# A hybrid transformer block on one core: weight sums taken one from the other, own tiles for four u columns, E tables on VectorE alone, output tables of the scan built in a later stage

## The chip, the core and the metric

The kernel runs on one core of a Trainium2 chip. The metric is the device time of one execution in microseconds (us). The core has a matrix engine (TensorE, PE in the rows; PEld are its weight loads), VectorE (DVE), ScalarE (ACT), GpSimd (POOL) and a queue engine (SP) that here issues every transfer in program order.

## The reference, cut to what matters

One layer on 1024 latent tokens and 256 context tokens, model width 1024, in float32:

```python
x = half_step_ffn(x, mods[0:3], ffn1_g_pre, ffn1_g_post, ffn1_w_gu, ffn1_w_down)
ctx = half_step_ffn(ctx, mods_c[0:3], ...same weights...)
disc = [s5_discretise(...) for d in range(2)]          # scan tables of 32 groups, 64 states
p = modulate(rms_norm(x, mix_g_pre), mods[3], mods[4]) @ w_in     # and the same for ctx
bg, cg, v, u = split(p)
y_conv = bg * grid_short_conv(cg * v, conv_w)
y_ssm = s5_readout(u, s5_states(u, disc, h0s), disc, ssm_d, w_glu, b_glu)
x = x + mods[5] * rms_norm(concat([y_conv, y_ssm]) @ w_out, mix_g_post)
x = half_step_ffn(x, mods[6:9], ffn2_g_pre, ffn2_g_post, ffn2_w_gu, ffn2_w_down)
# half_step_ffn: h @ w_gu -> g, u (2816 each); (silu(g) * u) @ w_down; norm, gate, add
```

## The kernel before

The latents' two FFNs use a seven-product scheme (Strassen's kind) on 2x2 blocks: for each *feature tile* f (128 columns of g and the same of u, 22 tiles) and each product m = 1 to 7, `g_lat` (L661) makes one weight operand of 128x512 in `prep` (L737) and multiplies it with a combination of the tokens' blocks in `prod` (L767). With g0, g1 the two row halves of a g tile and u0, u1 of a u tile, the operand is g0 for m=1, g1 for m=2, u0+u1 for m=5, u0+u1-g0 for m=6, g1-(u0+u1-g0) for m=3, g0-u0 for m=7, u1 for m=4. An operand is normally split into a high part (copied by ScalarE, `w<-t` or `w<-wr`) and a low part (VectorE, `w<-t,w`), and a product is 12 matmuls.

At the start of each FFN the normed tokens are not yet split, so the first four features run their products 1, 2, 5, 3 (the *early* ones, in the order m by m) with unsplit float32 operands: 4 matmuls each, in two passes, so 8 rows a product (`ps<-z,wr` for m=1 and 2, `ps<-z,t` for m=5 and 3). Meanwhile VectorE combines and splits the tokens' blocks (*hops*, rows `z<-z,z` and `z<-z`). Raw weights lie in four rotating buffers `wr` of 512 KB; the first FFN gives the four early u tiles buffers of their own (`z`, by `apart_u=True`, loaded by `u_load`), the second reloads them into `wr`.

`self.sums` holds u0+u1 of a feature; for the early features it is dropped after each use:

```python
                if m == 3 or f < ne:
                    sums.pop(f)
```

Around the products run other pieces of work as *fill* (generators that are stepped between products; `SP` sets how many fill steps pass between two steps of `s5_params`):

- `s5_params` (L1180 on) during the latents' first FFN makes the tables of the scan. Its last big part is the E table: 8 blocks of 6 operations of 128x512 (`tb<-tb`), the even blocks on VectorE, the odd ones on GpSimd. All blocks use the same two buffers, and each half is stored to DRAM (`pd<-tb`, 256 KB).
- `s5_prep` (L1399) during the context's first FFN (`g_ctx`, 128x256 matmuls) makes the B tables, then small transfers that lay out a Toeplitz table (`gd<-z`, `td<-gd`), then the output (C) tables: 4 blocks of 6 operations of 128x1024 (`z<-z,z`), alternately on VectorE and GpSimd, each with two stores of 512 KB (`pd<-z`).
- `u_lat` (L1501) projects the latents to u: 8 groups of 24 matmuls; beside it the context's tokens are normed, transposed and split (`ctx_in`, rows `z<-z,sy`, then `ps<-ident,z`, then `z<-t,z`). After it come `u_ctx` and the scan's pairs, which read the tables from `pd`.

Most of the order of instructions on each engine comes from the tile framework's scheduler; at the start of the first FFN VectorE and TensorE keep the program's order.

Of the kernel before, what the change touches and what calls it, by code (L numbers as in the profile page):

```python
# [68 lines left out]
class Kernel:  # L69
# [111 lines left out]
    def setup(self):  # L181
# [16 lines left out]
        self.pd = self.t(dr, [PAIRS, P, TO], "pd")  # L198
        self.pwd = self.t(dr, [P, D], "pwd")
        self.brd = self.t(dr, [P, D], "brd")  # L200
        self.gd = self.t(dr, [H, G, 15, H], "gd")
        self.td = self.t(dr, [P, G, P], "td")
        self.ud = self.t(dr, [G * H, T8, CL], "ud")
# [456 lines left out]
    def g_lat(self, wgu, hb, hr, sd, fills, early, late, held, apart_u=False):  # L660
# [73 lines left out]
        def prep(f, m):  # L734
            v = {
                side + str(q): raws[f, side][:, 4 * q : 4 * q + 4, :].rearrange("p k n -> p (k n)")
                for side in A[m] for q in range(2)  # L737
            }
            if m in (1, 2, 4):
                x = v[{1: "g0", 2: "g1", 4: "u1"}[m]]  # L740
            elif m == 7:
                x = self.t2()
                self.sub(x, v["g0"], v["u0"])
            else:
                x = sums.get(f)
                if x is None:
                    x = sums[f] = self.t2()
                    self.add(x, v["u0"], v["u1"])
                    have = 5
                else:  # L750
                    have = at_sum[f]
                if m in (6, 3) and have == 5:
                    self.sub(x, x, v["g0"])
                    have = 6
                if m == 3:
                    self.sub(x, v["g1"], x)
                    have = 3
                at_sum[f] = have
                if m == 3 or f < ne:
                    sums.pop(f)  # L760
            wops[f, m] = x if (f, m) in early else self.wop(x)

# [74 lines left out]
        def prepare(n, eager=True):  # L837
            nonlocal done
            while done < min(n, len(seq)):
                fetch(done)  # L840
                if any((seq[done][0], side) not in raws for side in A[seq[done][1]]):
                    break
                prep(*seq[done])
                done += 1
                if eager:
                    fetch(None)
# [327 lines left out]
    def s5_params(self):  # L1174
# [160 lines left out]
        for b in range(8):  # L1335
            gs = slice(4 * b, 4 * b + 4)
            er, ei, xt = (
                u.rearrange("p (a m n) -> p a m n", a=4, m=4) for u in (ee[:, :512], ee[:, 512:], arena[:, :512])
            )
            shp = [P, 4, 4, 32]  # L1340
            x0 = e32[0][:, gs, :].unsqueeze(2).to_broadcast(shp)
            x1 = e32[1][:, gs, :].unsqueeze(2).to_broadcast(shp)
            v0 = vv[:, 0, :, gs].rearrange("p m a -> p a m").unsqueeze(3).to_broadcast(shp)
            v1 = vv[:, 1, :, gs].rearrange("p m a -> p a m").unsqueeze(3).to_broadcast(shp)
            self.cmul(er, ei, x0, x1, v0, v1, xt, pl if b % 2 else None)
            for r, m in ((0, er), (1, ei)):
                c0 = EO + 256 * r
                self.load(
                    pdv[:, 2 * b : 2 * b + 2, c0 : c0 + 256], m.rearrange("p (a q) m n -> p a (q m n)", q=2)
                )  # L1350
            yield
# [30 lines left out]
    def s5_prep(self):  # L1382
# [82 lines left out]
        for t in range(T8):  # L1465
            r = slice(t * H, t * H + H)
            self.load(self.td[r], self.gd[:, :, 7 - t : 15 - t].rearrange("h g l k -> h g (l k)"))
            if t % TY == TY - 1:
                yield
        for o in range(4):  # L1470
            gs = slice(8 * o, 8 * o + 8)
            mr, mi, xt = slot(shp), slot(shp), slot(shp)
            prb, pib = power(1, 0, gs), power(1, 1, gs)
            cr_ = ct[:, 0, gs, :].unsqueeze(2).to_broadcast(shp)
            ci_ = ct[:, 1, gs, :].unsqueeze(2).to_broadcast(shp)
            e = pl if o % 2 else None
            self.mul(mr, cr_, prb, e)
            self.mul(xt, ci_, pib, e)
            self.add(mr, mr, xt, e)
            yield  # L1480
            self.mul(mi, ci_, prb, e)
            self.mul(xt, cr_, pib, e)
            self.sub(mi, mi, xt, e)
            for r, m in ((0, mr), (1, mi)):
                c0 = CO + 256 * r
                self.load(
# [228 lines left out]
    def run(self):  # L1715
# [199 lines left out]
        u = self.tb.rearrange("p (g c) -> p g c", g=G)  # L1915
        cx = ctx_in()
        next(cx)
        for _ in itertools.chain(self.u_lat(mhi, mlo, 0, u), self.u_lat(mhi, mlo, 1, u)):
            next(cx, None)
        for _ in cx:  # L1920
            pass
        self.u_ctx(chi2, clo2)
# [100 lines left out]
        order2 = [(f, m) for m in (1, 2, 5, 3) for f in range(4)]  # L2023
        tb = [self.ta() for _ in range(3)]
        held = {f: {1: halves(tb[f])[0], 2: halves(tb[f])[1], 0: [tb[f]]} for f in range(3)}
        ffn = self.g_lat(i["ffn2_w_gu"][0], hb, hr, self.sd[1], (0, 0, 1, 1, 0, 1, 0), order2, 3, held)
        next(ffn)
        for _ in range(4):
            self.g_fetch()
# [10 lines left out]
        ss.append(spl(3))  # L2040
        acc = self.out_group(ss[2], wo2)
        next(p)
        ssa = self.squares(part[:4])
        for _ in range(4):
            self.g_prep()
# [15 lines left out]
        self.eager = True  # L2061
        for _ in range(4):
            self.g_prod(4, 8)
        bl[1] = self.normer(part[4:], ssa, *ab)
        for _ in range(4):
            self.g_prod(4, 99)
        act = dict(h=lambda: next(h), p=lambda: self.g_prod(4, 99))
# [52 lines left out]
FW = 22  # L2120
FN = (2, 2, 1, 1, 2, 2, 2)
GAP = 6
SP = (1, 2)
UN2 = 3
EARLY2 = 4
TAIL = 3
# [47 lines left out]
```

## Time and profile before

| | us |
|---|---|
| three runs | 2076.4, 2077.2, 2079.46 (median 2077.2) |
| profiled execution, own time | 2077.89 |
| its span (first to last instruction) | 2076.1 |
| TensorE busy | 1961.8 (94%) |
| VectorE busy | 1433.3 (69%) |
| ScalarE / GpSimd busy | 825.3 / 191.3 |

The span is what the rows cover; 1.8 us of the execution's own time lie outside it. The share of busy time is an average over stages with different limits, so the places where TensorE waits are read one by one.

### The profile page before, as it was taken

What the parts mean: (1) busy time and instruction counts of PE and PEld (TensorE: products, weight loads), DVE (VectorE), ACT (ScalarE), POOL (GpSimd) and SP (SyncE); (2) the same over time, 40 slices, a digit from 0 to 9 for tenths busy, and PEclk for the clock granted to TensorE, in tenths of its full rate; (3) what the DMA queues carried; (4) which work ended last, traced back from release to release, by engine and by line L of the source; (5) the groups of instructions that cost most, each with busy time, mean ns of one, the idle gap of its engine ahead of it and who ended that gap; (6) DMA issues with size and microseconds to landing.
All of it is one profiled execution on the core that took longest, in us unless ns stands there. A gap on an engine that the chain in (4) does not pass through costs nothing. (4 is left out here: it accounts for less than half of the span.)

```text
span 2076.1 us, 25812 instructions
## 1 busy us (share of the span) xinstructions
PE 1961.8 (94%) x9364; PEld 1562.7 (75%) x9364; DVE 1433.3 (69%) x2532; ACT 825.3 (40%) x1459; POOL 191.3 (9%) x106
## 2 busy tenths in 40 slices
PE   7899999989898999999998899997999999999997
PEld 3477778867898877777887778763788888887775
DVE  1874469787766679787528985486865555577977
ACT  5433333423343345566532334353333333334543
POOL 0000000040347000000003430010000000000000
PEclk9999999999999999999999999999999999999999
DMA  9167632445579977476665533134632322267554
GB/s 325 31 218 249 240 137 72 132 127 167 172 222 268 294 249 251 147 259 224 180 207 170 182 112 122 53 130 122 203 122 81 100 73 82 87 254 267 198 182 162
DMA packets 334059, 356.78 MB, mean 172 GB/s; under 512 B 47024, under 2 KB 248428, under 8 KB 333932
## 3 DMA queue, kind: packets, MB, share of 16 engines
q1 hardware_dynamic: 331628, 346.75, 51.4%
q10 hardware_dynamic: 2304, 8.39, 1.0%
q8 instruction: 73, 1.20, 0.2%
q14 instruction: 54, 0.44, 0.1%
HBM read 282.97 MB, written 74.17 MB: 172 GB/s over the span
## 5 line engine op out<-in xcount | busy, mean ns | idle before, releaser
L51 PE MATMUL ps<-z,w 128*128 128x512 f32 (+1 forms) x5328 | 1151.2, 377 | 39.6 <-DVE w L51 13.1
L51 PEld LDWEIGHTS ps<-z,w 128*128 128x128 f32 x5328 | 937.7, 192 | 236.4 <-DVE w L51 14.9
L51 PE MATMUL ps<-w,w 128*128 128x512 f32 x1848 | 427.3, 392 | 16.3 <-DVE w L51 9.7
L51 PEld LDWEIGHTS ps<-w,w 128*128 128x128 f32 x1848 | 346.4, 188 | 95.6 <-DVE w L51 14.7
L51 ACT ACTIVATE w<-wr 128x512 fp32r<-128x512 f32 (+1 forms) x270 | 206.6, 767 | 348.4 <-PE ps L51 281.7
L51 DVE TENSOR_TENSOR w<-wr,w 128x512 fp32r<-128x512 f32 (+1 forms) x264 | 246.9, 937 | 117.4 <-ACT w L51 110.8
L51 ACT ACTIVATE w<-t 128x512 fp32r<-128x512 f32 x292 | 177.1, 626 | 213.4 <-DVE t L51 129.9
L51 DVE TENSOR_TENSOR w<-t,w 128x512 fp32r<-128x512 f32 x292 | 198.6, 691 | 77.0 <-ACT w L51 76.6
L51 DVE TENSOR_TENSOR t<-t,ps 128x512 f32<-128x512 f32 x150 | 102.4, 684 | 97.6 <-PE ps L51 94.5
L51 PE MATMUL ps<-z,t 128*128 128x512 f32 x512 | 148.0, 449 | 11.4 <-DVE t L51 10.3
L51 ACT ACTIVATE t<-ps 128x512 f32<-128x512 f32 (+2 forms) x143 | 77.4, 542 | 166.3 <-PE ps L51 162.8
L51 PEld LDWEIGHTS ps<-z,t 128*128 128x128 f32 x512 | 96.8, 190 | 60.8 <-issue 36.2
L51 ACT ACTIVATE w<-z 128x512 fp32r<-128x512 f32 x110 | 69.6, 632 | 146.2 <-PE ps L51 144.0
L51 DVE TENSOR_TENSOR z<-z,z 128x512 fp32r<-128x512 f32 (+3 forms) x127 | 106.6, 869 | 15.5 <-ACT z L51 11.6
L51 DVE TENSOR_TENSOR t<-wr 128x512 f32<-128x512 f32 x140 | 94.2, 686 | 32.2 <-DMA wr<-in_ffn_w_gu 18.1
L51 ACT ACTIVATE t<-z 128x1024 bf16<-128x1024 f32 (+3 forms) x132 | 75.5, 605 | 47.2 <-DVE z L51 30.8
L51 DVE TENSOR_TENSOR w<-z,w 128x512 fp32r<-128x512 f32 x110 | 75.5, 686 | 26.6 <-ACT w L51 26.4
L51 POOL TENSOR_TENSOR z<-z,z 128x1024 f32<-128x1024 f32 x24 | 79.2, 3320 | 76.3 <-PE ps L51 42.0
L51 ACT ACTIVATE t<-t 128x512 f32<-128x512 f32 (+1 forms) x83 | 51.7, 623 | 78.6 <-DVE t L51 78.2
L51 DVE TENSOR_TENSOR z<-t,ps 128x512 f32<-128x512 f32 (+1 forms) x52 | 29.8, 573 | 64.9 <-PE ps L51 64.3
L51 POOL TENSOR_TENSOR tb<-tb 128x512 f32<-128x512 f32 x24 | 33.6, 1412 | 435.4 <-DMA sd<-z 409.0
L51 ACT ACTIVATE z<-z 128x512 fp32r<-128x512 f32 (+2 forms) x76 | 48.3, 673 | 56.7 <-DVE z L51 56.7
(121 smaller groups left out, 1402.1 us busy)
## 6 DMA issues: line engine op xcount, KB each, us to landing
wr<-in_ffn_w_gu SPq DMA_DIRECT2D x146, 512.0 KB, 4.1
wr<-in_ffn_w_down SPq DMA_DIRECT2D x198, 256.0 KB, 4.2
tb<-in_w_ada SPq DMA_DIRECT2D x56, 512.0 KB, 4.5
sd<-z SPq DMA_DIRECT2D x44, 512.0 KB, 3.0
z<-sd SPq DMA_DIRECT2D x88, 256.0 KB, 5.4
wr<-in_ffn_w_down SPq DMA_DIRECT2D x22, 512.0 KB, 4.9
wr<-in_w_in SPq DMA_DIRECT2D x20, 512.0 KB, 4.0
z<-in_w_ada SPq DMA_DIRECT2D x16, 512.0 KB, 6.3
```

Of the source, the lines that this page charges most:

```text
L51: r = f(*a, **kw)
```

## The change

Five parts. (1) In `prep` an early feature keeps its sum from m=5 on: m=3 works it over in place (two operations, before three), and m=6 is made back from m=3's result (one operation, before two). A new condition in `prepare` holds m=3 and m=6 back until the products that read the tile were issued. (2) The second FFN gets `apart_u=True` too: its first four u tiles are loaded early into buffers of their own. (3) The E table is made on VectorE alone, in halves of three operations, with two fill steps between halves. (4) The C tables move from `s5_prep` into a new generator `s5_ctab` that is stepped beside `u_lat`, all on VectorE; its inputs go through DRAM (a new `ctd`, 512 KB, and half of `pwd`). (5) In the second FFN the last four token tiles are scaled by ScalarE instead of VectorE.

```diff
+        self.ctd = self.t(dr, [P, D], "ctd")
...
+                if m == 6 and have == 3:
+                    self.sub(x, v["g1"], x)
+                    have = 6
                 if m in (6, 3) and have == 5:
                     self.sub(x, x, v["g0"])
...
-                if m == 3 or f < ne:
+                if m == (6 if f < ne else 3):
                     sums.pop(f)
...
-                if any((seq[done][0], side) not in raws for side in A[seq[done][1]]):
+                f, m = seq[done]
+                if any((f, side) not in raws for side in A[m]):
+                    break
+                if f < ne and m in (3, 6) and left[f] & {5, 3 if m == 6 else 5}:
                     break
...
-            self.cmul(er, ei, x0, x1, v0, v1, xt, pl if b % 2 else None)
+            self.mul(er, x0, v0)
+            self.mul(xt, x1, v1)
+            self.sub(er, er, xt)
+            yield
+            self.mul(ei, x0, v1)
+            self.mul(xt, x1, v0)
+            self.add(ei, ei, xt)
...
+        self.load(self.ctd, ct.rearrange("p r a h -> p (r a h)"))
+
+    def s5_ctab(self):
+        slot = lambda shape: self.t(self.zp, shape, "z")
+        pw, ct = slot([P, 2, T8, 32]), slot([P, 2, 32, H])
+        self.load(pw.rearrange("p r t a -> p (r t a)"), self.pwd[:, 512:])
+        self.load(ct.rearrange("p r a h -> p (r a h)"), self.ctd)
...
         for o in range(4):
...
-            e = pl if o % 2 else None
-            self.mul(mr, cr_, prb, e)
-            self.mul(xt, ci_, pib, e)
-            self.add(mr, mr, xt, e)
+            self.mul(mr, cr_, prb)
+            self.mul(xt, ci_, pib)
+            self.add(mr, mr, xt)
             yield
...
+        ctab = self.s5_ctab()
         for _ in itertools.chain(self.u_lat(mhi, mlo, 0, u), self.u_lat(mhi, mlo, 1, u)):
             next(cx, None)
+            next(ctab, None)
...
-        ffn = self.g_lat(i["ffn2_w_gu"][0], hb, hr, self.sd[1], (0, 0, 1, 1, 0, 1, 0), order2, 3, held)
+        ffn = self.g_lat(i["ffn2_w_gu"][0], hb, hr, self.sd[1], (0, 0, 1, 1, 0, 1, 0), order2, 3, held, True)
...
+        for _ in range(4):
+            self.u_load()
...
-        bl[1] = self.normer(part[4:], ssa, *ab)
+        self.scale(part[4:], self.rsq(ssa), nc.scalar)
+        bl[1] = self.blocks(part[4:], *ab)
...
-SP = (1, 2)
+SP = (1,)
```

How it moves instructions is shown at three places, all on VectorE.

First FFN, from the last u sum of m=3 on (`t` are the operands, `z_265` an own u tile, `wr` raw weights, `ps` products). Before:

```order
L51 TENSOR_TENSOR t_232_677<-z_265 128x512
L51 TENSOR_TENSOR t_232_677<-t_232_677,wr_5_76 128x512
L51 TENSOR_TENSOR t_232_677<-wr_5_76,t_232_677 128x512
L51 TENSOR_TENSOR tb_72<-tb_72,ps_683 128x512
L51 TENSOR_TENSOR t_235_694<-t_222_640,ps_689 128x512
L51 TENSOR_TENSOR z_541<-z_541 128x512
L51 TENSOR_TENSOR z_697<-z_540,z_697 128x512
L51 TENSOR_TENSOR z_700<-z_541,z_700 128x512
L51 TENSOR_TENSOR t_238_703<-wr_5_76 128x512
L51 TENSOR_TENSOR t_238_703<-t_238_703,wr_2_73 128x512
L51 TENSOR_TENSOR w_706<-t_238_703,w_706 128x512
```

Now:

```order
L51 TENSOR_TENSOR t_217_617<-t_217_617,wr_5_76 128x512
L51 TENSOR_TENSOR t_217_617<-wr_5_76,t_217_617 128x512
L51 TENSOR_TENSOR tb_72<-tb_72,ps_676 128x512
L51 TENSOR_TENSOR t_232_687<-t_223_641,ps_682 128x512
L51 TENSOR_TENSOR z_542<-z_542 128x512
L51 TENSOR_TENSOR z_690<-z_541,z_690 128x512
L51 TENSOR_TENSOR z_693<-z_542,z_693 128x512
L51 TENSOR_TENSOR t_194_521<-wr_2_73,t_194_521 128x512
L51 TENSOR_TENSOR w_697<-t_194_521,w_697 128x512
```

The sum ahead of m=3 (`t_232_677<-z_265`) and the one ahead of m=6 (`t_238_703<-wr_5_76`) are gone; the adds of products (`<-...,ps`) stand where they stood.

Beside `u_lat`, around the scale of the context's two token tiles (`TENSOR_SCALAR z<-z,sy`; `z_8453,z_8452` are the inputs of the C tables, `w` a weight split, `z_8377<-t` the context's split). Before:

```order
L51 SCALAR_TENSOR_TENSOR sy_8598<-sq_8596,sy_8597 128x2
L51 TENSOR_SCALAR z_7802<-z_7802,sy_8598 128x1024
L51 TENSOR_SCALAR z_7803<-z_7803,sy_8598 128x1024
L51 TENSOR_TENSOR w_8635<-wr_4_75,w_8634 128x1024
L51 TENSOR_TENSOR w_8818<-wr_5_76,w_8817 128x1024
L51 TENSOR_TENSOR z_8435<-t_1374_8690,z_8433 128x256
```

Now:

```order
L51 TENSOR_TENSOR z_8632<-z_8632,z_8634 128x1024
L51 SCALAR_TENSOR_TENSOR sy_8554<-sq_8553,sy_8551 128x2
L51 TENSOR_TENSOR z_8634<-z_8453,z_8452 128x1024
L51 TENSOR_TENSOR sq_8553<-sy_8554 128x2
L51 SCALAR_TENSOR_TENSOR sq_8553<-sq_8553,sv_8550 128x2
L51 SCALAR_TENSOR_TENSOR sy_8555<-sq_8553,sy_8554 128x2
L51 TENSOR_SCALAR z_7744<-z_7744,sy_8555 128x1024
L51 TENSOR_SCALAR z_7745<-z_7745,sy_8555 128x1024
L51 TENSOR_TENSOR w_8841<-wr_2_73,w_8840 128x1024
L51 TENSOR_TENSOR z_8377<-t_1366_8664,z_8375 128x256
L51 TENSOR_TENSOR z_8633<-z_8453,z_8452 128x1024
L51 TENSOR_TENSOR z_8709<-z_8453,z_8452 128x1024
```

Sixteen of the 24 C operations and two weight splits now stand between the context's residual and its scale, seven more between its first and last splits.

Second FFN, where the operands of m=3 are made (`t_1941`, `t_1947`, `t_1950` before; now `t_1907`, `t_1909`, `t_1911`, `t_1913`). Before:

```order
L51 TENSOR_TENSOR t_1941_11712<-wr_3_74,t_1941_11712 128x512
L51 TENSOR_TENSOR t_1947_11736<-wr_3_74 128x512
L51 TENSOR_TENSOR t_1949_11747<-tb_72,ps_11742 128x512
L51 TENSOR_TENSOR t_1950_11749<-wr_4_75 128x512
L51 TENSOR_TENSOR t_1952_11760<-t_1901_11552,ps_11755 128x512
L51 TENSOR_TENSOR t_1947_11736<-t_1947_11736,wr_2_73 128x512
L51 TENSOR_TENSOR t_1950_11749<-t_1950_11749,wr_5_76 128x512
L51 TENSOR_TENSOR t_1947_11736<-wr_2_73,t_1947_11736 128x512
L51 TENSOR_TENSOR t_1950_11749<-wr_5_76,t_1950_11749 128x512
```

Now:

```order
L51 TENSOR_TENSOR t_1947_11736<-t_1900_11550,ps_11731 128x512
L51 TENSOR_TENSOR t_1913_11598<-t_1913_11598,wr_2_73 128x512
L51 TENSOR_TENSOR z_11392<-z_11611,z_11392 128x512
L51 TENSOR_TENSOR z_11391<-z_11391 128x512
L51 TENSOR_TENSOR z_11800<-z_11391,z_11800 128x512
L51 TENSOR_TENSOR t_1907_11571<-wr_3_74,t_1907_11571 128x512
L51 TENSOR_TENSOR t_1909_11580<-wr_4_75,t_1909_11580 128x512
L51 TENSOR_TENSOR t_1911_11589<-wr_5_76,t_1911_11589 128x512
L51 TENSOR_TENSOR t_1913_11598<-wr_2_73,t_1913_11598 128x512
```

The sums from `wr` are gone from here (made earlier, from own tiles), and the four operands, which were made one after the other as weights came, now end together behind 38 rows from the first hop of m=5.

## Rows read from the trace of the kernel before

**Rows 1.** The page: the engines' busy time, share of the span, instructions.
```profile
PE 1961.8 (94%) x9364; PEld 1562.7 (75%) x9364; DVE 1433.3 (69%) x2532; ACT 825.3 (40%) x1459; POOL 191.3 (9%) x106
```

**Rows 2.** Stretches: length; busy PE, PEld, DVE, ACT, POOL; clock; DMA; GB/s.
```profile
99.00:107.00 8.00, 7.31 (x16) 4.92 (x17) 8.00 (x14) 4.69 (x8) 0.00 (x0) 0.50 0.28 83
404.00:471.00 67.00, 59.78 (x245) 47.71 (x244) 55.80 (x68) 21.20 (x37) 33.65 (x24) 0.95 0.45 130
650.00:700.00 50.00, 37.62 (x272) 35.90 (x271) 37.93 (x30) 14.38 (x19) 27.24 (x6) 0.90 0.96 296
1000.00:1050.00 50.00, 50.00 (x225) 40.35 (x224) 20.83 (x36) 20.59 (x34) 2.44 (x1) 1.00 0.54 156
1600.00:1650.00 50.00, 50.00 (x218) 40.35 (x217) 28.16 (x48) 17.77 (x32) 0.00 (x0) 1.00 0.28 92
```

**Rows 3.** PE in order of time, first FFN: start, length, count, wait before.
```profile
65.00 27.63 PE L51 MATMUL ps<-z,t 128*128 128x512 f32 x64
99.01 3.66 PE L51 MATMUL ps<-z,w 128*128 128x512 f32 x7 [6.37 <-ACT z L51]
```

**Rows 4.** DVE in order of time, the same place.
```profile
83.64 0.68 DVE L51 TENSOR_TENSOR t<-z 128x512 f32<-128x512 f32 x1
...
86.28 0.68 DVE L51 TENSOR_TENSOR t<-t,ps 128x512 f32<-128x512 f32 x1
...
89.58 0.69 DVE L51 TENSOR_TENSOR t<-wr 128x512 f32<-128x512 f32 x1 [0.62 <-DMA wr<-in_ffn_w_gu]
...
90.31 0.69 DVE L51 TENSOR_TENSOR t<-t,wr 128x512 f32<-128x512 f32 x1
...
97.61 2.67 DVE L51 TENSOR_TENSOR z<-z,z 128x512 f32<-128x512 f32 x4
```

**Rows 5.** PE in order of time, 425 to 510.
```profile
432.00 5.85 PE L51 MATMUL ps<-z,w 128*128 128x512 f32 x24 [2.25 <-ACT t L51]
442.81 50.22 PE L51 MATMUL ps<-z,w 128*128 128x512 f32 x204 [4.97 <-DVE t L51]
```

**Rows 6.** E table: POOL's group, DVE beside it, the stores to landing.
```profile
L51 POOL TENSOR_TENSOR tb<-tb 128x512 f32<-128x512 f32 x24 | 33.6, 1412 | 435.4 <-DMA sd<-z 409.0 <-DVE tb L51 16.2 <-DMA pd<-tb 9.4
418.56 1.77 DVE L51 TENSOR_TENSOR t<-wr,wr 128x512 f32<-128x512 f32 x1
426.82 1.29 DVE L51 TENSOR_TENSOR tb<-tb 128x512 f32<-128x512 f32 x2 [2.69 <-DMA pd<-tb]
pd<-tb SPq DMA_DIRECT2D x16, 256.0 KB, 3.2
```

**Rows 7.** 640 to 700: who waited for whom, total, times, longest.
```profile
PE ps L51 <- ACT w L51: 6.8, 4, 3.6
PE ps L51 <- DVE w L51: 5.5, 4, 3.2
ACT w L51 <- DMA wr<-in_ffn_w_gu: 16.6, 4, 7.8
```

**Rows 8.** C operations on DVE, 600 to 700: min/median/max in ns.
```profile
L51 DVE TENSOR_TENSOR z<-z,z x16: 1205/1206/3061, 602.3 to 678.3; 128x1024 f32<-128x1024 f32 x15, 16x512 f32<-16x512 f32 x1
```

**Rows 9.** DVE, then PE, in order of time beside `u_lat`.
```profile
1020.12 1.41 DVE L51 TENSOR_SCALAR z<-z,sy 128x1024 f32<-128x1024 f32 x2
1054.98 2.10 DVE L51 TENSOR_TENSOR z<-t,z 128x256 fp32r<-128x256 f32 x6 [2.30 <-ACT z L51]
1038.81 0.38 PE L51 MATMUL ps<-ident,z 128*128 128x128 f32 x2
1055.00 5.24 PE L51 MATMUL ps<-z,w 128*128 128x256 f32 x41 [0.99 <-ACT z L51]
```

**Rows 10.** PE in order of time, start of the second FFN.
```profile
1412.88 17.51 PE L51 MATMUL ps<-z,t 128*128 128x512 f32 x40 [0.98 <-DVE t L51]
1437.56 5.72 PE L51 MATMUL ps<-z,t 128*128 128x512 f32 x8 [7.16 <-DVE t L51]
1445.46 7.13 PE L51 MATMUL ps<-z,t 128*128 128x512 f32 x16 [2.18 <-DVE t L51]
1456.31 5.91 PE L51 MATMUL ps<-z,w 128*128 128x512 f32 x13 [1.61 <-DVE w L51]
```

More of the change, by code (lines that the diff above doesn't have):

```diff
@@ L1469, in s5_prep @@
                 yield
+        self.load(self.ctd, ct.rearrange("p r a h -> p (r a h)"))
[4 more added lines that the diff above has]
+        self.load(ct.rearrange("p r a h -> p (r a h)"), self.ctd)
+        pdv = self.pd.rearrange("a p w -> p a w")
+        shp = [P, 8, T8, H]
+        yield
         for o in range(4):
@@ L1472, in s5_prep @@
             mr, mi, xt = slot(shp), slot(shp), slot(shp)
-            prb, pib = power(1, 0, gs), power(1, 1, gs)
+            prb, pib = (pw[:, r, :, gs].rearrange("p t a -> p a t").unsqueeze(3).to_broadcast(shp) for r in range(2))
             cr_ = ct[:, 0, gs, :].unsqueeze(2).to_broadcast(shp)
             ci_ = ct[:, 1, gs, :].unsqueeze(2).to_broadcast(shp)
-            e = pl if o % 2 else None
-            self.mul(mr, cr_, prb, e)
-            self.mul(xt, ci_, pib, e)
-            self.add(mr, mr, xt, e)
+            self.mul(mr, cr_, prb)
+            self.mul(xt, ci_, pib)
+            self.add(mr, mr, xt)
             yield
-            self.mul(mi, ci_, prb, e)
-            self.mul(xt, cr_, pib, e)
-            self.sub(mi, mi, xt, e)
+            self.mul(mi, ci_, prb)
+            self.mul(xt, cr_, pib)
+            self.sub(mi, mi, xt)
             for r, m in ((0, mr), (1, mi)):
@@ L1917, in run @@
         next(cx)
+        ctab = self.s5_ctab()
         for _ in itertools.chain(self.u_lat(mhi, mlo, 0, u), self.u_lat(mhi, mlo, 1, u)):
             next(cx, None)
+            next(ctab, None)
+        for _ in ctab:
+            pass
         for _ in cx:
```

## Prediction, made before the changed kernel was run

> **What bounds the kernel now.** I read the page first: TensorE is busy 94% of the span [rows 1]. Then the stretches: from 1600 to 1650 it starts 218 matmuls of 128x512 in 50.00 us without a pause, 0.23 us each [rows 2]. That is the rate to hold every other stage against: the kernel is bound by TensorE wherever operands are there, so an edit is worth what it gives back at the few places where TensorE waits, or runs at the lower clock after a wait. Work taken from VectorE elsewhere is worth nothing. Then I read TensorE's rows in order of time for those places. Four lie where the change works.
>
> - First FFN, 92.6 to 99.0: after the early products (64 rows from 65.00, 27.63 us) TensorE waits 6.37 us for the hop of the next operand [rows 3]. From 99 to 107 the granted clock is 0.50 (the 1.2 GHz level), 16 matmuls in 8.00 us, so 8.00 - 16 x 0.23 = 4.3 us more are lost [rows 2].
> - E table, 404 to 471: waits of 2.25 and 4.97 us [rows 5]; 245 matmuls at 0.23 would be 56.4 us of the 67.0, so 10.6 us are lost there, clock included [rows 2].
> - Context's FFN, 640 to 700: 6.8 + 5.5 = 12.3 us of waits, and behind them ScalarE, idle 16.6 us for weights [rows 7]; from 650 to 700 the DMA engines are 0.96 busy at 296 GB/s, with a clock of 0.90 [rows 2].
> - Second FFN, 1412 to 1462: waits of 0.98, 7.16, 2.18 and 1.61 us; and the 13 matmuls from 1456.31 take 5.91 us where 13 x 0.23 is 3.0 [rows 10].
>
> Beside `u_lat` (1000 to 1050) TensorE has no wait, and VectorE works 20.83 of 50 us [rows 2]. That is the cover that the moved C tables are put under.
>
> **First FFN: 3 us.** Until TensorE restarts, VectorE loses four u sums of m=3 and the first sums of two m=6 operands, 0.60 to 0.73 us each (89.58 to 90.31 for one of m=6, with 0.62 us ahead for a reloaded u tile that m=6 no longer reads) [rows 4]. But not all of it counts. The add at 86.28 takes the m=3 product of the second feature, and that product ends after 48 of the 64 early rows, at 65.00 + 48 x 0.43 = 85.7 [rows 3]. It runs 0.6 us behind it, so the four sums ahead (2.4 us) save only 0.5. After it two sums (1.4) and the 0.62 go: 2.5 together, TensorE restarts near 96.5. Two more m=6 sums (1.2) fall later, while VectorE still has no pause. In-place work adds no wait here: m=5 of the first feature ends 16 rows after 65.00. So 2.5 to 3.7; I take 3. Bounds 1 (something else is late) and 6.4 (the whole wait).
>
> **E table: 5 us.** VectorE takes over 24 operations. The trace has their kind on GpSimd at 1412 ns, 33.6 us in all [rows 6]. In the same 67 us VectorE is busy 55.80 us with 68 instructions, 0.82 each, where two in a row without GpSimd's work take 1.29, so 0.60 for each further one, and one beside it took 1.77 [rows 2, 6]. So 68 x 0.22 = 15 us of stretch go and 24 x 0.60 = 14.4 come: VectorE's time is a wash, and what falls away is the uneven pace. In the new order one latents' feature takes 30 or 31 VectorE rows here, 31 x 0.60 = 18.6 us, against 84 matmuls x 0.23 = 19.3 of TensorE: 0.7 us to spare. What can eat it: each half is written into a buffer whose last store must have landed. 256 KB take 3.2 us to landing, VectorE waited 2.69 for one [rows 6], and in the new order the next writer stands 5 to 8 rows (2.4 to 4.2 us between) after the last. I count up to 1 us a wait, about 5 a feature against 0.7 to spare, for three features, less what the operands made ahead cover: 5 of the 10.6 us stay. Gain 5; bounds -4 (every wait lands on TensorE) and 10.
>
> The Trainium skill (SBUF — State Buffer, Who interferes with whom) says that a VectorE instruction with two SBUF inputs and a GpSimd one that reads SBUF exclude each other, and the later one waits for the whole of the other. The 1.77 us row agrees in kind. By that rule alone all 33.6 us of GpSimd's time block VectorE, and the whole 10.6 us would come back.
>
> **Context's FFN: 9 us.** Out of the full stretch go eight stores of 512 KB (4.2 MB, 14 us at 296 GB/s) and GpSimd's 27.24 us; a store of 512 KB comes [rows 2]. In the new order of SP's queue two weight loads also stand ahead of the eight `td<-gd` transfers which in before stood behind them. The `gd` and `td` transfers stay. I take three quarters of the 12.3 us of waits [rows 7]; bounds 3 (the small transfers were it) and 14 (the clock comes back too).
>
> **Beside u_lat: -3 us.** 24 operations at 1.2 us [rows 8] are 29 us of VectorE in a stage with 29 us to spare in 50 [rows 2]. By the order, 16 of them and two weight splits come before the context's scale. It ran at 1020.12; 18 x 1.2 = 21.6 later is 1041.7, and some 2 less where VectorE had been waiting, against transposes at 1038.81 [rows 9]: 1 to 3 us late. Behind it four more precede the second split and three the rest, so the last splits, at 1054.98 before, end up to 2 later; partly the same delay, so I take 3 for both. Bounds 0, and 8 (the C stores, 4.2 MB more, hold back SP's queue and weights behind them).
>
> **Second FFN: 8 us.** Early sums move to where VectorE waits for products, four scales go to ScalarE, m=6 reuses m=3's tile, and no reload stands in the way. TensorE starts m=5 near 1411.7 with 32 rows x 0.43 = 13.8, so until 1425.5. But all four m=3 operands now come behind 38 VectorE rows from 1409.7. The first 12 wait for ScalarE as before (until about 1417.7), 26 x 0.60 more give 1433.4. So the first m=3 product starts near 1434, a *longer* wait, 8.5 us, than the 7.16 now, since before one of the four went ahead of it. From there 32 rows run through, with 2 us lost to the clock as at 1437.56 (8 rows in 5.72 us where 3.4 would do), until 1450; before, 1445.46 + 7.13 = 1452.6 [rows 10]. Then the waits until 1456.31 fall away, since the m=6 operands are made while m=3 runs, and the 13 slow matmuls may run at full clock (2.9). 1456.3 less two matmuls is 1455.5; to 1450 that is 5.5, and with most of the clock 8. Bounds 2 and 12.
>
> The pairs of the scan are reordered by a few rows: 0, within 2.
>
> **Sum.** 3 + 5 + 9 - 3 + 8 = 22. The profiled execution took 2077.89, of which 2076.1 are its span and 1.8 lie outside: 2055.9. The median of the runs is 0.7 below the profiled one, so 2055.
>
> **Rivals.**
> (a) VectorE becomes the bound in the E stage, with its order as the price: every store wait costs. 16 waits of the full 3.2 us are 51 us; from about 2 us each (32, less 10 for operands made ahead) they take back all 22. That is slower than before, for example 2.8 each: 45 - 10 = 35 lost where I count a gain of 5, so 2055 + 5 + 35 = 2095. For it: 2.69 in [rows 6], and SP's queue, in which stores stand behind weight loads that wait for a buffer. Against it: 5 to 8 rows between, and a median landing of 3.2. A mild form (-4) gives 2064.
> (b) GpSimd's share was the whole E loss, as the exclusion would have it: 10.6 instead of 5, 2050. For it: the long rows only stand beside GpSimd's. Against it: the wait for the store.
> (c) The change doesn't do what it says in the context's FFN: `gd` and `td` made the waits. 3 instead of 9: 2061. For it: ScalarE's longest waits, 7.8 us [rows 7], lie right behind the `td` transfers. Against it: twice as many bytes in the stores.
> (d) The second FFN only swaps one wait for another, since the in-place m=3 must come behind m=5: 2 instead of 8, 2061.
> (e) The C tables are late, with 8 for 3: 2060; the context's chain has no slack from 1038.81 on.
>
> **How the numbers follow.** The forecast with its own spread (2048 to 2062) 0.50; (a) mild 0.10 and full 0.07; (b) 0.11; (c) 0.09; (d) 0.07; (e) 0.06. The likeliest is 2055. Leaving out the full form of (a) and the outer half of the mild one and of (b), the range is 2046 to 2066. About 0.2% (4 us) is what a measurement can tell from no change. Cases above 2081: (a) full, 0.07, and two or three mishaps together, 0.02: slower 0.09. Within 4 us of before: (a) mild with (c), (d) or (e): 0.05. Faster: 0.86.
>
> **What would show it.** First FFN: the wait at 99.01 shrinks to about 4. E stage: no VectorE row of this shape over 0.75 us, waits only for `pd<-tb`. Context's FFN: the waits of ScalarE for `wr` fall from 16.6 to under 6. `u_lat`: transposes wait 1 to 2 us for VectorE. Second FFN: one wait of 8 to 9 us between m=5 and m=3, then none to speak of. I am wrong if the E stage has several waits over 2 us, or if the stretch after the `td` transfers keeps its waits.

## The result, and the profile after

The changed kernel takes 2044.4 us (median of 4 runs, 2042.5 to 2046.4) against 2078.1 before (median of 4): a ratio of 0.984, 95% interval 0.982 to 0.986, so 34 us faster. The forecast was 2055, with a range of 2046 to 2066: right in sign, 11 us too cautious, and the measured time lies just below the range.

Both kernels issue 9364 matmuls in the same order of stages, so the n-th of one can be set against the n-th of the other. The table shows how much earlier than before TensorE comes out of each stage (stage bounds in us of the trace of before, gains in us). Three profiles of the changed kernel stand in it (own times 2045.3, 2040.2 and 2039.4), all set against the one profile of before.

```
stage (us of before)               forecast   1st    2nd    3rd
60-130    first FFN, start            +3     -1.1   +0.2   +0.1
404-490   E table                     +5    +10.0  +10.0  +10.0
490-520   behind the E table           0     +8.5   +8.5   +8.5
520-640   B tables                     0     -2.6   -1.4   -2.0
640-700   context's FFN               +9     +9.9  +13.2  +13.1
1000-1060 beside u_lat                -3     -2.8   -4.0   -2.5
1060-1405 u_ctx, the scan's pairs      0     +2.2   +2.2   +2.0
1405-1470 second FFN, start           +8     +8.6   +8.1   +8.8
all else                               0     +0.1   +1.1   +0.7
```

The page's line of busy times: GpSimd went from 191.3 us [rows 1] to 111.5; TensorE is busy for 12.4 us less with the same matmuls.

```profile
PE 1949.4 (95%) x9364; PEld 1554.5 (76%) x9364; DVE 1419.7 (69%) x2548; ACT 830.8 (41%) x1463; POOL 111.5 (5%) x70
```

TensorE in order of time, start of the first FFN, E table and second FFN (start, length, count, wait before; the last row of each of the three goes on past what is shown):

```profile
96.69 0.79 PE L51 MATMUL ps<-z,w 128*128 128x512 f32 x1 [3.73 <-ACT z L51]
98.97 2.93 PE L51 MATMUL ps<-z,w 128*128 128x512 f32 x6 [1.49 <-DVE z L51]
102.58 4.22 PE L51 MATMUL ps<-z,w 128*128 128x512 f32 x17 [0.68 <-DVE z L51]
109.80 20.46 PE L51 MATMUL ps<-z,w 128*128 128x512 f32 x81 [3.00 <-DVE tb L51]
...
394.71 95.83 PE L51 MATMUL ps<-z,w 128*128 128x512 f32 x410
...
1409.78 15.73 PE L51 MATMUL ps<-z,t 128*128 128x512 f32 x32 [8.83 <-DVE t L51]
1424.95 35.33 PE L51 MATMUL ps<-z,w 128*128 128x512 f32 x149
```

Against [rows 3] the first wait of the first FFN fell from 6.37 to 3.73 us, as forecast, but three more follow it, of which 1.49 and 3.00 are new. Against [rows 5] the E stage has no stop at all. Against [rows 10] the second FFN has one wait of 8.83 us where four stood.

VectorE's rows in the E stage, 395 to 450, the first three groups:

```profile
L51 DVE TENSOR_TENSOR tb<-tb 128x512 f32<-128x512 f32 x41 | 27.2, 684 | 0.9 <-DMA pd<-tb 0.6 <-DMA tb<-in_ssm_b_re 0.3
L51 DVE TENSOR_TENSOR w<-wr,w 128x512 fp32r<-128x512 f32 x10 | 6.8, 685 | 0.5 <-ACT w L51 0.5
L51 DVE TENSOR_TENSOR t<-t,ps 128x512 f32<-128x512 f32 x8 | 5.5, 682 | 1.5 <-PE ps L51 1.5
```

Every group of 128x512 now takes 0.68 us, and the stores are waited for 0.6 us in this stretch.

### The profile page after: what moved, and what is told of

It reads as the page before. It is cut to its first block, busy times and chain, and to the rows that moved or that the text cites. A ratio compares the mean times of both kernels' runs of the same rounds, so it can differ in the third digit from the quotient of the medians.

```text
span 2043.5 us, 25754 instructions
## 1 busy us (share of the span) xinstructions
PE 1949.4 (95%) x9364; PEld 1554.5 (76%) x9364; DVE 1419.7 (69%) x2548; ACT 830.8 (41%) x1463; POOL 111.5 (5%) x70
## 4 chain that ended last, share of the span: by engine, by line
PE 74%; DVE 15%; DMA 5%; issue 2%; ACT 2%; SPq 1%; POOL 1%; DVEq 0%; ACTq 0%; POOLq 0%
PE ps L51 74%; DVE z L51 6%; DVE t L51 5%; DVE w L51 3%; DMA wr<-in_ffn_w_down 1%; SPq L51 1%; DMA wr<-in_ffn_w_gu 1%; ACT t L51 1%; DMA z<-in_w_ada 1%; ACT w L51 1%; ACT z L51 1%; DMA z<-in_x 0%; POOL t L51 0%; DVE sy L51 0%; DMA wr<-t2d 0%
## 5 line engine op out<-in xcount | busy, mean ns | idle before, releaser
L51 PEld LDWEIGHTS ps<-w,w 128*128 128x128 f32 x1848 | 346.6, 188 | 93.8 <-DVE w L51 15.1
L51 DVE TENSOR_TENSOR w<-wr,w 128x512 fp32r<-128x512 f32 (+1 forms) x264 | 234.3, 889 | 117.5 <-ACT w L51 114.8
L51 DVE TENSOR_TENSOR z<-z,z 128x512 fp32r<-128x512 f32 (+3 forms) x139 | 114.3, 856 | 16.7 <-ACT z L51 11.7
L51 DVE TENSOR_TENSOR t<-wr 128x512 f32<-128x512 f32 x124 | 83.6, 686 | 20.3 <-DMA wr<-in_ffn_w_down 13.4
L51 PE MATMUL ps<-w,t 128*128 128x512 f32 x264 | 64.4, 401 | 1.9 <-DVE w L51 1.3
L51 ACT ACTIVATE z<-ps 128x512 f32<-128x512 f32 x74 | 41.6, 595 | 56.6 <-PE ps L51 56.5
```

Of the source, the lines that this page charges most:

```text
L51: r = f(*a, **kw)
```

## The experiments

The stage readings below come from the same pairing of matmuls, as gains over the kernel before. Three stages scatter from run to run: the first FFN's start (the 16 profiles with the new sums lie between -2.6 and +0.4), the context's FFN, and the place beside `u_lat` (-6.1 and -2.7 in two profiles of one kernel). A single profile says little of them.

### The E table

**As it was.** The old blocks, GpSimd's half and fill steps, the rest as changed:

```diff
-            self.mul(er, x0, v0)
...
+            self.cmul(er, ei, x0, x1, v0, v1, xt, pl if b % 2 else None)
-SP = (1,)
+SP = (1, 2)
```

> The changed kernel with the E table alone as it was: whole blocks of six operations, the odd blocks on GpSimd, and the old number of fill steps. Theory A (the E table is worth the whole of what the E stage and the place right behind it gained, 10 + 8.5 us, since the table ends some 9 us earlier and the next tables with it): about 2063, with the waits of 2.25 and 4.97 us at 432 and 443 back, and those of some 2 us at 495 and 505 too. Theory B (my forecast's term: 5 us, and the place behind it belongs to another part): about 2049, with the E waits back but no loss of clock from 490 to 520.

Measured 2067.3 us (2065.9 to 2073.8; 0.995 of before, 0.993 to 0.997). The E stage gains 1.1 in place of 10.0, the place behind it -0.3 in place of 8.5, and the context's FFN 6.9 in place of 10 to 13 (the profiled execution took 2073.8, the other three at most 2067.6). Theory A, and a little more: the part is worth some 23 us here, the largest of the five.

**Halves and pace kept, odd blocks on GpSimd.**

```diff
-            self.mul(er, x0, v0)
+            e = pl if b % 2 else None
+            self.mul(er, x0, v0, e)
```

(and so for the other five operations of a block)

> The changed kernel with its E table in halves and its fill steps as they are, but the odd blocks on GpSimd again: 24 operations go back from VectorE to GpSimd, and nothing else moves. Theory A (GpSimd beside VectorE is the cause of the old loss: what runs there makes VectorE's rows longer and the feature uneven): about 2054 to 2063, with VectorE rows of 0.8 us and more in the E stage and several waits of TensorE over 2 us. Theory B (the pace of the halves and the fill steps is the cause, and the engine matters little): 2044 to 2047, TensorE without a stop as in the changed kernel. Theory C (VectorE is at its limit in the changed kernel): faster than it, about 2040.

Measured 2056.3 us (2054.8 to 2058.5; 0.990, 0.989 to 0.992). The E stage loses 2.1 where the changed kernel gains 10.0; the place behind it keeps all its 8.5. So the engine makes the E stage, and not the place behind it. Four of VectorE's groups there:

```profile
L51 DVE TENSOR_TENSOR w<-wr,w 128x512 fp32r<-128x512 f32 x7 | 8.5, 1209 | 0.2 <-ACT w L51 0.2
L51 DVE TENSOR_TENSOR t<-t,ps 128x512 f32<-128x512 f32 x7 | 4.8, 679 | 0.0
L51 DVE TENSOR_TENSOR t<-t,wr 128x512 f32<-128x512 f32 x3 | 4.0, 1345 | 0.0
L51 DVE TENSOR_TENSOR t<-wr,wr 128x512 f32<-128x512 f32 x3 | 4.0, 1341 | 0.0
```

In the three groups here with both inputs in SBUF the rows take 1.2 to 1.35 us on the mean (the two other large ones, `tb<-tb` and `w<-t,w`, 0.75 and 0.88); rows with one input in PSUM (`t<-t,ps`) still 0.68.

**Halves on VectorE, old fill steps.**

```diff
-SP = (1,)
+SP = (1, 2)
```

> The changed kernel with its E table in halves on VectorE, but the old number of fill steps between them (one and two by turns instead of one). Theory A (the quicker steps are what brings the tables behind E forward and takes the waits at 495 and 505 away): no loss in the E stage itself, and 8 us lost from 490 to 520, about 2052. Theory B (GpSimd's absence ends E earlier by itself): 2044 to 2046, both places as in the changed kernel.

Measured 2054.4 us (2050.6 to 2056.6; 0.989, 0.986 to 0.991). The E stage keeps its 10.0; the place behind gains 4.5 instead of 8.5, between the two theories. The rest of the loss lies in the context's FFN (7.2) and the pairs (0.6). So of the 8.5 the quicker steps make 4.0. With the old steps, the other 4.5 came with the halves or with VectorE in GpSimd's place: the whole blocks half on GpSimd have nothing of it, and halves half on GpSimd with the old steps were not run. In the trace TensorE's wait of 2.18 us for a VectorE operand is gone, and one of 1.60 us for VectorE ahead of the transposes stays at 493.72.

**Useless GpSimd work beside the changed E table.**

```diff
+            for q in range(6 * (b % 2)):
+                self.mul(du, x0[:, :2], v0[:, :2], pl)
```

(before each half; `du` is a part of `arena` that is not in use)

> The changed kernel, VectorE's 48 operations of the E table and their order untouched, with 48 GpSimd operations of 128x256 added that read the tables of E and write a buffer nobody else uses: work without a use, which nobody waits for, some 34 us of GpSimd. Theory A (what GpSimd runs beside VectorE stretches VectorE's rows with two inputs from SBUF): rows of 1.0 us and more in place of 0.68 while GpSimd works, waits of TensorE back, 5 to 12 us lost from the start of GpSimd's work on; 2048 to 2056. Theory B (in the old kernel the blocks by turns and the buffers they held made the loss): rows of 0.68, no loss, 2040 to 2046.

Measured 2058.1 us (one run). GpSimd ran the 48 operations from 380.93 on, 0.96 us each; VectorE's order was the same. From 130 to 490 the kernel loses 4.5 us where the changed one gains 9.5. VectorE's groups from 395 to 450:

```profile
L51 DVE TENSOR_TENSOR tb<-tb 128x512 f32<-128x512 f32 x32 | 27.1, 871 | 0.0
L51 DVE TENSOR_TENSOR w<-wr,w 128x512 fp32r<-128x512 f32 x6 | 5.7, 970 | 0.0
L51 DVE TENSOR_TENSOR t<-t,ps 128x512 f32<-128x512 f32 x7 | 4.8, 679 | 1.2 <-PE ps L51 1.2
```

and TensorE there:

```profile
400.14 14.21 PE L51 MATMUL ps<-z,w 128*128 128x512 f32 x60 [3.46 <-DVE t L51]
415.13 5.87 PE L51 MATMUL ps<-z,w 128*128 128x512 f32 x24 [0.78 <-ACT t L51]
427.78 75.28 PE L51 MATMUL ps<-z,w 128*128 128x512 f32 x312 [6.79 <-DVE t L51]
```

Theory A. Nobody waits for this work, VectorE itself waits for nothing from 395 to 430, and yet its rows grow from 0.68 to 0.87 to 0.97 and TensorE waits again. Rows with a PSUM input stay at 0.68.

### The C tables

**Back in the context's FFN, half on GpSimd** (the old loop behind the `td` transfers, no `s5_ctab`), and a second profile of it:

```diff
-        self.load(self.ctd, ct.rearrange("p r a h -> p (r a h)"))
+            e = pl if o % 2 else None
+            self.mul(mr, cr_, prb, e)
...
-            next(ctab, None)
```

> The changed kernel with the C tables back in the context's FFN, alternately on VectorE and GpSimd as before, and nothing of them beside the projections of u. By my forecast's terms (9 us gained in the context's FFN, 3 us lost beside the projections): slower by 6, about 2050 to 2051; by the stages that I read from the two traces (10 and 3) by 7, 2051. Rival (c), by which the small transfers made the waits: slower by 0 to 2, 2044 to 2046, with ScalarE's waits for raw weights the same in both.

> The same kernel as with the C tables back in the context's FFN, for a second profile, since the profiled execution of the first took 7 us less than its other three. If those 7 us are lost between 640 and 700, GpSimd's half and the stores cost 6 to 7 us more there than the first profile showed; if elsewhere, they have to do with something else.

Measured 2051.8 us (2044.4 to 2052.1; 0.987, 0.985 to 0.989) and 2049.3. The context's FFN gains 6.7 and 4.2 in the two profiles instead of 10 to 13; beside the projections +0.2 and +0.1. So moving the tables is worth 3 to 9 in one place and costs 3 to 4 in the other: the forecast's -3 holds, and its 9 is the upper end. With the tables back, the place still gains 4 to 7 over before, which is not theirs. The first profile's execution took 2044.4, where the other three took 2051.7 to 2052.1; the second lost its 5 us in the first FFN (2.7) and the context's (2.5), two of the stages that scatter.

**Back there, all on VectorE.**

```diff
-            e = pl if o % 2 else None
+            e = None
```

> The changed kernel with the C tables back in the context's FFN, but all on VectorE: the eight stores of 512 KB are there again, GpSimd's 17 us for its half of them are not. Theory A (the stores fill the transfers and the weights come late): as slow as with GpSimd's half, about 2051, TensorE's waits of 12 us behind ScalarE's and VectorE's weight parts back. Theory B (GpSimd's share and its late stores did it): 2042 to 2046, those waits as small as in the changed kernel, and the 3 us beside the projections won besides.

Measured 2046.2 us (2043.5 to 2048.8; 0.985, 0.984 to 0.987). In the place named the loss is there, as by theory A: the context's FFN gains only 3.5 (in a profile of 2048.8, the longest of the four), and TensorE's waits from 600 to 680 are back:

```profile
PE ps L51 <- ACT w L51: 6.6, 4, 3.2
PE ps L51 <- DVE w L51: 3.4, 1, 3.4
```

where the changed kernel has

```profile
PE ps L51 <- ACT w L51: 3.0, 1, 3.0
PE ps L51 <- DVE w L51: 1.2, 2, 0.8
```

The profile's busy share of the DMA engines reads 1.02 from 640 to 690, against 0.88. But the three long waits of TensorE, then VectorE's rows ahead of the third, and SP's first C store show that the stores did not make them:

```profile
640.11 0.80 PE L51 MATMUL ps<-z,w 128*128 128x256 f32 x2 [3.22 <-ACT w L51]
642.90 0.80 PE L51 MATMUL ps<-z,w 128*128 128x256 f32 x2 [2.00 <-ACT w L51]
647.11 11.06 PE L51 MATMUL ps<-z,w 128*128 128x256 f32 x70 [3.41 <-DVE w L51]
...
633.37 12.55 DVE L51 TENSOR_TENSOR z<-z,z 128x1024 f32<-128x1024 f32 x11
645.85 1.21 DVE L51 TENSOR_TENSOR w<-wr,w 128x1024 fp32r<-128x1024 f32 x1
...
648.22 0.37 SPq L51 DMA_DIRECT2D pd<-z  x1
```

All three waits are over when the first C store is issued, at 648.22. The third is for a weight part that stands behind eleven C rows on VectorE; the first two end when ScalarE has copied raw weights, loaded at 634.04 and 636.01 behind `gd` transfers. So theory A's cause, the stores, is not borne out. In the sum this kernel is nearly as fast as the changed one, since nothing is lost beside the projections.

**The steps later.** First only in the loop, with the draining of the C steps still ahead of the context's rest (the old sums of the first FFN stand in this kernel too):

```diff
-            next(cx, None)
-            next(ctab, None)
+            if next(cx, 0) == 0:
+                next(ctab, None)
```

> Two undoings far apart, read by stage: the u sums of the first FFN as before, and the C tables' steps beside the projections only begun when the context's steps are through. By the single run with the old sums (2038.8, of which only 0.2 to 1.3 us lie in the first FFN) the first is worth 1 us and the rest of its distance is the spread of the context's FFN from run to run. The second: by theory A (the 18 VectorE operations ahead of the context's scale made the 3 us) the stretch from 1000 to 1060 gains 2 to 3 and the scan's pairs lose 0 to 2. Together 2040 to 2042. By theory B (the 3 us are the traffic of C stores and inputs) 2043 to 2044.

Measured 2060.7 us (2060.6 to 2064.4; 0.993, 0.991 to 0.994). This put the whole of the C tables *ahead* of the context's split, and 19.0 us were lost from 1000 to 1060, with one wait of 11.84 us. It tests the opposite of what was meant, and agrees with theory A in it: what stands ahead on VectorE is what TensorE waits for. The mended order drains the context's steps first:

```diff
+        for _ in cx:
+            pass
         for _ in ctab:
             pass
-        for _ in cx:
-            pass
```

> The steps of the C tables follow those of the context's norm, transposes and split, mended: in the earlier kernel of this kind the rest of the context's steps still stood behind all of the C tables, so it tested the opposite. Theory A (the 18 VectorE operations ahead of the context's scale made the loss of 3 us): the stretch from 1000 to 1060 loses 0 to 1 instead of 2.8, the pairs lose 0 to 4 as the tables come later; 2041 to 2045. Theory B (traffic and inputs of the C tables made it): 3 us lost there as before.

Measured 2058.5 us (one run). From 1000 to 1060 it gains 0.2 instead of losing 2.5 to 4.0, as by theory A (the C stores come later here too, from 1053.0 on, so this run alone doesn't set their traffic apart from the order). But the pairs lose 15.1, as they now wait for tables:

```profile
1076.77 2.47 PE L51 MATMUL ps<-tb,z 128*128 128x160 f32 x8 [7.38 <-DMA z<-pd]
```

I had put that price at 0 to 4. Of the orders tried, the loss of 3 us is the cheapest.

### The sums of the first FFN

```diff
-                if m == (6 if f < ne else 3):
+                if m == (6 if f < ne and keep else 3) or f < ne and not keep:
```

(`keep` is off in the first FFN here; it also switches the new condition in `prepare`)

> The changed kernel with the old u sums in the first FFN alone: m=3 and m=6 of the early features make their sum anew. By my forecast's term (the sums taken one from the other gain 3 us): the stretch from 60 to 130 is 3 us longer, 2047. By the two traces (a loss of 1 between 60 and 130): it is 1 us shorter, 2043. The wait at 99 would be 6.4 again instead of 3.7 in both; they differ in whether the three waits behind it (1.5, 0.7 and 3.0) go.

Measured 2038.8 us (one run), of which at most 1.3 lie here: the stage reads +0.2, and 0.0 and -0.3 in two more kernels with the old sums. The new sums give -2.6 to +0.4. So they bring nothing, and the single time is a good draw of the context's FFN (15.6).

### The second FFN

Three undoings: no own u tiles; sums made anew (`keep` off there); the last scales on VectorE.

```diff
-ffn = self.g_lat(i["ffn2_w_gu"][0], hb, hr, self.sd[1], (0, 0, 1, 1, 0, 1, 0), order2, 3, held, True)
+ffn = self.g_lat(i["ffn2_w_gu"][0], hb, hr, self.sd[1], (0, 0, 1, 1, 0, 1, 0), order2, 3, held)
```

> The changed kernel with the four early u tiles of the second FFN reloaded into the rotating buffers, as before; the sums taken one from the other and ScalarE's scales stay. Theory A (own tiles bring the 8.6 us): about 2052, one of the m=3 operands ahead of the others again, and waits of 2 us behind m=3. Theory B (what m=6 no longer makes brings them): 2044 to 2047.

> The changed kernel with the u sums of the second FFN's early features made anew for m=3 and m=6 as before, from own u tiles; the first FFN keeps the changed way. Theory A (what VectorE no longer does between m=5 and m=6 is the gain): the wait between m=5 and m=3 grows by four to eight rows of 0.7, or the waits of 2.2 and 1.6 us behind m=3 come back: 2048 to 2050. Theory B (own tiles alone do it, since the sums are made while VectorE waits for products): 2044 to 2046.

> The changed kernel with the last four token tiles of the second FFN scaled by VectorE again: four rows of 128x1024, 0.7 to 1.2 us each, go back to VectorE ahead of the blocks. If VectorE is what the first products wait for, the second FFN starts 1 to 4 us later, 2046 to 2048; if ScalarE's scales only trade places with them, 2044 to 2045, or up to 2 less.

Single runs of 2049.6, 2042.8 and 2043.1 us; read by stage, 1405 to 1470 gains 1.3, 5.6 and 8.2 in place of 8.1 to 8.8. By these single profiles own tiles are worth 7, the sums 3 (together more than the 8.5, so they overlap; how was not tried), ScalarE's scales nothing that shows. Without the new sums:

```profile
1403.20 12.09 PE L51 MATMUL ps<-z,t 128*128 128x512 f32 x24 [5.73 <-DVE t L51]
1415.25 6.05 PE L51 MATMUL ps<-z,w 128*128 128x512 f32 x24
1424.30 55.92 PE L51 MATMUL ps<-z,w 128*128 128x512 f32 x228 [3.00 <-DVE t L51]
```

the wait splits in two, 5.73 and 3.00, together as long as the one of 8.83, and one of m=3's products goes ahead again.

### The same kernel again, and a faster one

> The changed kernel itself, for a second profile: the gain of the context's FFN was 10.0 us from 650 to 700 in its first one and 12.1 to 15.6 in five other kernels that are the same there. If that is the spread of the stage from run to run, the second profile shows some 12 to 13 there and four runs of 2040 to 2046; if it hangs on where the edits of the others shift the stage, it shows 10 again.

Measured 2043.0 us (2040.2 to 2046.3; 0.983, 0.981 to 0.986), with 13.2 in the context's FFN: spread from run to run.

If GpSimd's work stretches VectorE's rows beside the E table, it should do so beside the B tables too, where a wait of 5.72 us for VectorE stands at 544.56:

```diff
-            self.cmul(xr, xi, power(0, 0, gs), power(0, 1, gs), b0, b1, xt, pl if o % 2 else None)
+            self.cmul(xr, xi, power(0, 0, gs), power(0, 1, gs), b0, b1, xt, None)
```

> The changed kernel with the B tables of the context's FFN on VectorE alone too (before and after the change the odd ones of four blocks are on GpSimd, 12 operations of 128x1024). Theory A (what stretched VectorE's rows beside the E table stretches them here: its weight rows of 128x1024 mean 1.42 us from 520 to 700 where 1.2 is their time alone): the wait of 5.7 us for a VectorE weight part near 545, and the slow clock behind it, shrink, about 2038 to 2041. Theory B (VectorE has no room: 12 operations of 1.2 us are 14 us more in the same stage): 2044 to 2050.

> The changed kernel with B tables on VectorE alone and with the old u sums in the first FFN. If both effects add up (7 us for the B tables by their run's median against that of the changed kernel, 1 for the sums): 2036, and faster than the changed kernel beyond the spread of the runs.

> The kernel with the B tables on VectorE alone again, beside the changed kernel on one chip in five rounds: if it is faster, 2036 to 2040 against 2042 to 2045, with intervals that do not overlap.

> The changed kernel in five rounds, for that comparison: 2042 to 2045.

Measured 2037.5 us (2034.0 to 2040.6; 0.981, 0.979 to 0.983); with the old first sums as well 2040.3 (0.982, 0.979 to 0.984), so the sums add nothing. In five rounds on one chip 2038.0 (2036.1 to 2038.1; 0.981, 0.979 to 0.982) against 2043.2 for the changed kernel (four runs, 2039.4 to 2043.7; 0.983, 0.982 to 0.984). The runs of the two don't overlap, the intervals do by a hair: some 5 us faster. From 520 to 640 the three profiles gain 3.4 to 5.7 where the changed kernel lost 1.4 to 2.6. VectorE's groups from 520 to 600, changed kernel:

```profile
L51 DVE TENSOR_TENSOR w<-wr,w 128x1024 fp32r<-128x1024 f32 x20 | 32.8, 1642 | 14.3 <-ACT w L51 12.8 <-DMA z<-in_ssm_c_re 1.3
L51 DVE TENSOR_TENSOR z<-z,z 128x1024 f32<-128x1024 f32 x12 | 18.8, 1598 | 0.0
```

B tables on VectorE alone:

```profile
L51 DVE TENSOR_TENSOR w<-wr,w 128x1024 fp32r<-128x1024 f32 x21 | 25.7, 1223 | 11.9 <-ACT w L51 10.4 <-DMA z<-in_ssm_c_re 1.3
L51 DVE TENSOR_TENSOR z<-z,z 128x1024 f32<-128x1024 f32 x21 | 24.9, 1218 | 0.0
```

These 42 rows take 50.6 us where 32 took 51.6, and the wait at 544.56 is gone.

## Why the prediction was right and wrong

Three terms of the sum were wrong: the E table's waits for stores, the place behind it, which stood at nothing, and the first FFN. A fourth, the context's FFN, came out in size but not by its cause.

**E table: mis-sized, 5 for 10.** That VectorE has the time for all 48 operations was right. With the old fill steps (halves on VectorE) the table's first row starts at 408.8, before at 405.4 (in the changed kernel already at 387.6), and from 404 to 471, which holds the whole table in both, VectorE is busy 61.62 us with 102 rows, 0.60 each, under 289 matmuls of TensorE without a stop; before it was 55.80 us with 68 rows, 0.82 each, under 245 [rows 2]. The step that failed is "I count up to 1 us a wait, about 5 a feature against 0.7 to spare". The stores landed in 2.1 us in the median, 2.8 at most, where the median of before was 3.2 [rows 6], and VectorE waited 0.8 us in all, twice, from 380 to 480. With the old fill steps they took up to 3.5 us, and VectorE still waited only 0.7, so the rows between cover them. Nothing to speak of stayed of the 10.6 us. Rival (a) falls; rival (b) was right in its mechanism, shown from both sides: GpSimd's half put back costs 12 us in the stage, and GpSimd's useless work 14 from 130 to 490.

The Trainium skill (SBUF — State Buffer, Who interferes with whom) says that a VectorE instruction with two SBUF inputs contends with a GpSimd instruction that reads SBUF, and one with at most one SBUF input, outside its two-port modes, does not. The runs agree in both halves: 0.68 to 0.87 and more for the first kind, 0.68 unchanged for rows that take one input from PSUM. I had that rule and the row of 1.77 us, and gave more weight to the single wait of 2.69 us for a store.

**Behind the E table: a term that was missing, 8.5.** The waits of 2.18 at 495.21 and 2.24 at 504.81, and the low clock behind them (0.83 from 495 to 515), were in the trace of before, and I gave them to nobody. VectorE waited 5.94 us at 492.98 for a weight load that SP's queue issued behind the E stage's tail; in the changed kernel the tail ends some 9 us earlier against TensorE's work, and the same wait is 2.46. The runs show that 4.0 of the 8.5 hang on the fill steps; the rest came with the halves or the engine, and which of the transfers ahead counts most was not tried apart.

**Context's FFN: right in size, not by its cause.** 9.9 to 13.2 for 9, within 3 to 14. "Out of the full stretch go eight stores of 512 KB" was the reason, by weights that come late. ScalarE's waits for `wr` did not fall to under 6: in the same stage (600 to 690 in both traces) they are 14.1 us, before 16.6. And of the waits before, the two longest are not behind the C stores:

```profile
654.47 0.80 PE L51 MATMUL ps<-z,w 128*128 128x256 f32 x2 [3.64 <-ACT w L51]
678.46 14.27 PE L51 MATMUL ps<-z,w 128*128 128x256 f32 x118 [3.17 <-DVE w L51]
...
675.03 3.37 DVE L51 TENSOR_TENSOR w<-wr,w 128x1024 fp32r<-128x1024 f32 x1
...
660.88 1.58 SPq L51 DMA_DIRECT2D pd<-z  x1
```

The wait of 3.64 is over before the first C store is issued at 660.88; it ends with raw weights loaded behind the `gd` transfers. The wait of 3.17 is for a VectorE row that took 3.37 us beside GpSimd's C rows, where a row of its kind takes 1.21 at 679.79: the same stretch as in the E table. Of the waits, at most the 3.2 us for ScalarE between 663 and 668, beside the stores, can be theirs. So that 9 fitted is in part luck: the move is worth 3 to 9, in part by VectorE's rows, and 4 to 7 of the gain are there with the C tables back. What makes those was not found. With the old E table or the old fill steps this place gains only 7, but so does (7.3) the kernel with B tables on VectorE and the old first sums, which has the new E table; single profiles do not tie it to the E stage. Rival (c) does not fall: `gd` transfers stand ahead of the late weights before the change and with the C tables back on VectorE.

**Beside u_lat: right.** -2.5 to -4.0 for -3 (down to -6.1 in other kernels with the C tables there), TensorE waiting 1.20 us at the transposes, then 1.47 and 0.62. The order was the cause: VectorE has no pause of note from 999 to the scale at 1013.80, C rows among what it does, and with the C operations behind the context's chain the loss is gone. Rival (e) falls.

**First FFN: right at the head, wrong in the sum, 3 for about 0.** "TensorE restarts near 96.5": it did, at 96.69. But the 2.6 us of the shorter wait were given back within 13 us, by the trace in two rows of VectorE behind the head:

```profile
97.62 0.69 DVE L51 TENSOR_TENSOR t<-wr,t 128x512 f32<-128x512 f32 x1 [1.05 <-DMA wr<-in_ffn_w_gu]
...
109.07 0.68 DVE L51 TENSOR_TENSOR tb<-tb,ps 128x512 f32<-128x512 f32 x1
```

The new operand row waits for raw weights that no longer come in time, in front of the hop's low part, and the add of a product stands at 109.07 where it stood at 106.82, with five more rows between the weight parts and it; TensorE waits for each, 1.49 and up to 3.00. I had followed the queue to the head of the wait and no further.

**Second FFN: right.** One wait of 8.83 us for the 8.5 worked out, at 1409.78, and none behind; 8.1 to 8.8 for 8. Rival (d) falls.

**B tables and pairs.** -1.4 to -2.6 between 520 and 640, not in the sum, and not explained; 2.0 to 2.2 in the pairs, at the edge of "0, within 2" or just past it. In the kernels with GpSimd's half of the C or the E tables the pairs gain -0.3 to 0.3; the reason stays open.

With E at 10 and the place behind at 8.5 the sum would have been 22 + 13.5 = 35.5, and less the 3 of the first FFN 32.5: 2045.4 by the profiled run of before; in the first profile the other misses cancel.

## What to carry over

Work given to GpSimd isn't free for VectorE: look for VectorE rows of one shape that are longer beside GpSimd's rows and the same where an input comes from PSUM; if VectorE then does both in the same time, the offload never paid. Before you blame a store for a wait, see whether it was issued before the wait ended. Count a wait behind the last row that you shortened, not only at it: what is next in that engine's queue, and when its inputs land. Waits right behind a stage that gets shorter belong to the sum too.

## What the runs showed of the hardware

Beside a run of GpSimd operations of 128x512 (E table half on GpSimd), VectorE's rows of 128x512 with two SBUF inputs came out at 1.34 us, twice their 0.68, and GpSimd's own at 1.58 on the mean; no run shows GpSimd's rows without VectorE's beside them. At 128x1024, beside the B tables, rows of 1.22 us came to 1.60 on the mean. Where both engines had such rows without a pause, in the context's FFN of before, they ran in step: VectorE's began at 665.77, 668.73, 672.05 and 675.03 and took 3.0 to 3.4 us, GpSimd's began at 664.7, 667.7, 671.0 and 674.1 and took 3.0 to 3.4. That is not always so: the GpSimd row before these reads 17.1 us, from 645.6 on, while VectorE's C rows beside it went on at 1.2. In the context's FFN of the changed kernel, with the DMA engines 0.88 busy, the gain scattered by 3 us between profiles of one kernel.
